# A trunk of two attention layers: the order of issue as a list of 3107 numbers

## Chip, cores and metric

The kernel runs on one core of a Trainium2 chip. A core has five engines that each work off a queue of their own in order: TensorE (PE, matrix products), VectorE (DVE), ScalarE (ACT), GpSimd (POOL), and SyncE (SP), which here only issues DMA transfers. The metric is the device time of one execution in microseconds (us), the median of several runs; smaller is better.

## What is computed

The reference takes a sequence of 256 rows of 1024 float32 numbers through two layers, each with a residual, and a final RMS norm:

```python
c_act = jax.nn.silu(c)
for layer in range(2):
    ada = einsum('bd,de->be', c_act, w_ada[layer]) + b_ada[layer]
    shift, scale, gate = split(ada, 3)
    h = rms_norm(x, norm_g[layer]) * (1 + scale) + shift
    y = even_mixer(h, ...) if layer == 0 else odd_mixer(h, ...)
    x = x + gate * y
return rms_norm(x, final_g)

def even_mixer(h, ...):     # one input projection of width 2968
    oa = swa_sink_attention(qa, ka, va, sinks) * silu(za)       # 8 heads, window 128
    ob = nsa_attention(qb, kc, vc, ks, vs, kw, vw, gb) * silu(zb)  # 8 heads, compressed + selected + window
    return concat(oa, ob) @ w_out

def odd_mixer(h, ...):      # one input projection of width 4096
    q, k, v, z = split(h @ w_in)
    return (moba_attention(q, k, v) * silu(z)) @ w_out          # 16 heads of 64
```

With 256 rows the selected blocks and the window of the second branch cover all past rows, and the odd layer's attention is causal over one block.

## The kernel before

Everything is float32. A weight is loaded as float32 into a buffer `raw` (five buffers, by SP's queue). ACT casts it to a rounded high half `whi`, DVE subtracts that from it for a low half `wlo`, and each projection is made of three fp32r products per tile of 128 rows of depth (`mm3`):

```python
T.matmul(o, shi, mhi, start=first, stop=False)
T.matmul(o, shi, mlo, start=False, stop=False)
T.matmul(o, slo, mhi, start=False, stop=last)
```

The activations are halved in the same way (`hhi`, `hlo` for the layer's input, `ghi`, `glo` for the gated attention output). Scores (`ps_s<-qT`), attention outputs (`ps_o<-pT,vb` and the like), and the sums of the condition (`ps_m<-cz,..`, `ps_m<-ones,acc`) are plain fp32 products, in part on subdivided tiles of the PE array. Transposes go by PE into the bank `ps_pt`, and ACT copies them out.

The first layer's input projection runs in eight groups over depth (`start_prep`, `start_mm`): each loads a slice of the condition's weights `w_ada` (into `qT` buffers and into `gate`), makes shift and scale of 128 features (`shs`), makes `hhi` and `hlo` for them, splits 128 rows of the projection's weights, and adds its products to seven banks. Then come the attention of the first layer, two heads at a time (`attn_pair`), with the gated projections (`gated`) and the condition's later parts in between, its output projection, the second layer's input projection and attention in quads of heads (`attn_quad`), and the output projection. The gate of a layer is made by DVE as a weighted sum of weight rows into `acc`, a product with ones on PE into `ps_m`, and an addition to `gate` on DVE (`ada_gate`).

The output of a layer goes through `add_scaled`: DVE multiplies the bank by `gate` (`t<-ps_pj,gate`), adds that to the residual `xs`, and sums the squares for the norm. At the end of the second layer the 256 rows are two tiles of 128; for each, POOL raises the mean square to the power −1/2 (`inv_root`, `parts`), ACT scales 384 columns and DVE 640 (`TENSOR_SCALAR t<-xs,parts`), and two transfers store them.

No operation is issued where it is written. `T`, `V`, `A`, `G` and `Y` stand for the five engines, and each call goes to `Plan.record`, which keeps it with the set of earlier operations that it depends on (overlaps of buffers and banks). The buffers of a ring are handed out while the operations are recorded. At the end `Plan.issue` emits all 3107 of them in the order that `Plan.order` returns; the waits between engines follow from the dependencies. `order` is a list scheduler: it estimates each operation's duration (`_cost`) and the delay between engines (`LAT`), ranks operations by the longest path behind them, places them forward in time (`_forward`), ranks them anew from a backward pass (`_backward`), and after twelve rounds keeps the order with the smallest estimated end. `plan.head` marks the SP transfers of the first stage, which stay in order of recording, and `groups` are sets of operations that get one common rank. Since all calls are made in `issue` through what `record` kept, nearly all rows of the profile have one line, L146.

Of the kernel before, what the change touches and what calls it, by code (L numbers as in the profile page):

```python
# [32 lines left out]
RAW, HIB, LOB = 5, 4, 4  # L33
INIT = 3e38

class _Engine:
# [10 lines left out]
class Plan:  # L49

    MIX = 1.0
    ROUNDS = 12
    COLD = 4200.0
    LAT = {
        "pe": {"pe": 0.0, "act": 197.0, "dve": 196.0, "pool": 270.0},
        "act": {"pe": 260.0, "act": 127.0, "dve": 131.0, "pool": 61.0},
        "dve": {"pe": 256.0, "act": 128.0, "dve": 127.0, "pool": 155.0},
        "pool": {"pe": 200.0, "act": 61.0, "dve": 60.0, "pool": 96.0},  # L60
    }

    def __init__(self, nc):
        self.ops = []
        self.acc = {}
        self.masks = {}
        self.after = {}
        self.groups = []
        self.head = 0
        self.tensor = _Engine(self, "pe", nc.tensor)  # L70
        self.vector = _Engine(self, "dve", nc.vector)
        self.scalar = _Engine(self, "act", nc.scalar)
        self.gpsimd = _Engine(self, "pool", nc.gpsimd)
        self.sync = _Engine(self, "sp", nc.sync)
# [21 lines left out]
    def _space(ap):  # L96
        return str(ap.space).split(".")[-1]

    @staticmethod
    def _n(ap):  # L100
        n = 1
        for d in ap.shape[1:]:
            n *= d
        return n

    def fence(self, key):

        self.after[key] = [i for i, o in enumerate(self.ops) if o["key"] == key][-1:]
# [1 line left out]
    def group(self, ids):  # L110

        deps = set().union(*(self.ops[i]["deps"] for i in ids)) - set(ids)
        for i in ids:
            self.ops[i]["deps"] = self.ops[i]["deps"] | deps
        self.groups.append(ids)

    def record(self, eng, name, args, kw):
        outs = [args[0]] if args else []
# [13 lines left out]
        for nm, b, w in uses:  # L132
# [7 lines left out]
                keep.append((ob, ow, oi))  # L140
            keep.append((b, w, i))
            self.acc[nm] = keep
        dur, dma = self._cost(eng.key, name, outs, ins, kw)
        real = eng.real
        self.ops.append(
            dict(key=eng.key, dur=dur, dma=dma, deps=deps, prio=i, fn=lambda: getattr(real, name)(*args, **kw))  # L146
        )
        return i

    def _cost(self, key, name, outs, ins, kw):  # L150
        o = outs[0]
        n = self._n(o)
        if name == "dma_start":
            return 0.0, n * o.shape[0] * 4 / 360.0
        if key == "pe":
            if name == "transpose":
                return 109.0, 0
            if "tile_position" in kw:
                f = o.shape[0] / 128 * ins[0].shape[0] / 128
                return n * 4 / 2.4 * f + (22 if o.shape[0] == 32 else 4), 0  # L160
            if str(ins[0].dtype).endswith("float32r"):
                return max(n / 2.4 + 4.5, 109.0), 0
            return max(n * 4 / 2.4 + 8, 218.0), 0
        src = max([self._n(a) for a in ins] + [n])
        psum = any(self._space(a) == "PSUM" for a in ins + outs)
        nap = sum(1 for a in ins[1:] if self._n(a) == 1 and n > 1)
        if key == "act":
            return 0.833 * n + (51 if psum else 93) + 93 * nap + (93 if "accum_out" in kw else 0), 0
        if key == "dve":
            if name in ("tensor_copy", "tensor_scalar"):  # L170
                return n * (1.04 if psum else 0.53) + 69 + 62 * nap, 0
            if name == "reciprocal":
                return 60 + 8.4 * n, 0
            if name == "memset":
                return 60 + 0.6 * n, 0
            return src * 1.04 + 70 + 62 * nap, 0
        return (150 + 2.1 * n if name == "tensor_tensor" else 140 + 1.25 * n), 0

    def _lat(self, a, b):
        return 0.0 if a["dma"] else self.LAT[a["key"]].get(b["key"], 100.0)  # L180

    def order(self):

        ops = self.ops
        n = len(ops)
        self.succ = succ = [[] for _ in range(n)]
        for i, o in enumerate(ops):
            for d in o["deps"]:
                succ[d].append(i)
        tail = [0.0] * n  # L190
        for i in range(n - 1, -1, -1):
            o = ops[i]
            t = o["dur"] + (o["dma"] + 2000.0 if o["dma"] else 0.0)
            for j in succ[i]:
                tail[i] = max(tail[i], tail[j] + self._lat(o, ops[j]))
            tail[i] += t
        top = max(tail)
        prio = [(1.0 - self.MIX) * o["prio"] * top / n + self.MIX * (top - tail[i]) for i, o in enumerate(ops)]
        best = None
        for _ in range(self.ROUNDS):  # L200
            for ids in self.groups:
                first = min(prio[i] for i in ids)
                for i in ids:
                    prio[i] = first
            start, end = self._forward(prio)
            if best is None or max(end) < best[0]:
                best = (max(end), start, end)
            prio = self._backward(end)
        _, start, end = best
        for i, o in enumerate(ops):  # L210
            o["start"], o["end"] = start[i], end[i]
        return sorted(range(n), key=lambda i: (start[i], i))

    def _backward(self, end):

        ops = self.ops
        n = len(ops)
        top = max(end)
        left = [len(q) for q in self.succ]
        avail = [0.0] * n  # L220
        late = [0.0] * n
        free = {k: 0.0 for k in ("pe", "act", "dve", "pool", "dma")}
        ready = {k: {} for k in free}
        kind = ["dma" if o["dma"] else o["key"] for o in ops]
        for i in range(n):
            if left[i] == 0:
                ready[kind[i]][i] = 0.0
        for _ in range(n):
            t0, k = min((max(free[k], min(rd.values())), k) for k, rd in ready.items() if rd)
            i = min((j for j, a in ready[k].items() if a <= t0), key=lambda j: (-end[j], -j))  # L230
            ready[k].pop(i)
            o = ops[i]
            if o["dma"]:
                free[k] = max(t0, avail[i] + 1400.0) + o["dma"]
                done = free[k] + 1450.0
            else:
                free[k] = done = t0 + o["dur"]
            late[i] = top - done
            for d in o["deps"]:
                avail[d] = max(avail[d], done + self._lat(ops[d], o))  # L240
                left[d] -= 1
                if left[d] == 0:
                    ready[kind[d]][d] = avail[d]
        return late

    def _forward(self, prio):
        ops, succ = self.ops, self.succ
        n = len(ops)
        left = [len(o["deps"]) for o in ops]
        free = {k: 0.0 for k in ("pe", "act", "dve", "pool", "sp")}  # L250
        ready = {k: {} for k in free}
        avail = [0.0] * n
        start = [0.0] * n
        ends = [0.0] * n
        hw_free, dma_free = 0.0, 1600.0
        for i in range(n):
            if left[i] == 0:
                ready[ops[i]["key"]][i] = 0.0
        fifo = [i for i in range(n - 1, -1, -1) if ops[i]["key"] == "sp" and i < self.head]
        for _ in range(n):  # L260
            now = dict(ready)
            if fifo:
                now["sp"] = {fifo[-1]: avail[fifo[-1]]} if left[fifo[-1]] == 0 else {}
            t0, k = min((max(free[k], min(rd.values())), k) for k, rd in now.items() if rd)
            i = min((j for j, a in now[k].items() if a <= t0), key=lambda j: (prio[j], j))
            t0 = max(free[k], ready[k].pop(i))
            o = ops[i]
            if k == "sp" and fifo:
                fifo.pop()
            if o["dma"]:  # L270
                if k == "pool":
                    free[k] = t0 + 1000.0
                    issued = t0 + 1600.0
                else:
                    free[k] = hw_free = max(hw_free, t0) + 450.0
                    issued = hw_free + 1000.0
                dma_free = max(issued, dma_free) + o["dma"]
                end = dma_free + 1400.0
            else:
                dur = 2 * o["dur"] if k == "pe" and t0 < self.COLD else o["dur"]  # L280
                free[k] = end = t0 + dur
            start[i], ends[i] = t0, end
            for j in succ[i]:
                avail[j] = max(avail[j], end + self._lat(o, ops[j]))
                left[j] -= 1
                if left[j] == 0:
                    ready[ops[j]["key"]][j] = avail[j]
        return start, ends

    def issue(self):  # L290
        for i in self.order():
            r = self.ops[i]["fn"]()
            self.ops[i]["inst"] = r


@with_exitstack
# [466 lines left out]
        start_mm(g, *prep)  # L763
        prep = nxt

    plan.head = len(plan.ops)
    Y.dma_start(tb, tbl_b[:, :1056])
    snk = const([P, 16], "snk")
    A.dma_start(snk[:, 0:8], a_sinks[0:1, :].to_broadcast([P, 8]))
# [553 lines left out]
```

## Time and profile before

| | us |
|---|---|
| median of three runs | 320.14 (319.93 to 320.33) |
| the profiled execution | 320.77 |
| its span, first to last instruction | 319.0 |
| PE busy | 302.2 |
| DVE busy | 265.7 |
| ACT busy | 186.2 |
| POOL busy | 12.4 |
| mean granted clock of TensorE | 0.985 |

The span is the time from the first to the last instruction in the profile; the execution's own time is a little longer. Busy times are sums over the instructions of one engine. Matmuls overlap in the pipeline, so the durations of neighbouring matmul rows overlap too, and the pace of PE is read from the distance of their starts.

### The profile page before, as it was taken

The numbers are of one execution on the slowest core, as the hardware profiler recorded it, in microseconds if no ns is written. First come the engines' busy times: TensorE is split into PE (matmuls) and PEld (weight loads), VectorE is DVE, ScalarE is ACT, GpSimd is POOL, SyncE is SP. The second block draws the span as 40 slices with busy tenths as digits, with TensorE's granted clock in tenths as the row PEclk, the third lists the DMA queues.
The fourth block names the chain that finished last, engine by engine and source line by source line (L and its number), as shares of the span: only waits on it lengthen the run. The fifth ranks groups of instructions, "written<-read, shape, count | busy, mean of one in ns | idle before, by whom it ended". The sixth has DMA issues, their size and how long they took to land.

```text
span 319.0 us, 6319 instructions
## 1 busy us (share of the span) xinstructions
PE 302.2 (95%) x2246; PEld 252.8 (79%) x2246; DVE 265.7 (83%) x744; ACT 186.2 (58%) x481; POOL 12.4 (4%) x30
## 2 busy tenths in 40 slices
PE   8599998989999999999999999999999999999990
PEld 8286876888677577788887789998999998987880
DVE  0369798899999999998899686689989969997854
ACT  5434336773665669978344785256645768773601
POOL 5000000001000000000001000000000000000102
PEclk9959999999999999999999999999999999999998
DMA  6999999998994796437599956726779443405003
GB/s 201 321 319 297 316 325 352 342 358 283 353 351 157 228 349 217 133 134 262 181 283 282 356 180 237 221 83 225 217 217 341 133 153 130 135 3 198 0 2 132
DMA packets 71280, 71.85 MB, mean 225 GB/s; under 512 B 3080, under 2 KB 62928, under 8 KB 71248
## 3 DMA queue, kind: packets, MB, share of 16 engines
q1 hardware_dynamic: 70528, 70.90, 70.1%
q10 hardware_dynamic: 592, 0.48, 0.5%
q8 instruction: 18, 0.29, 0.4%
q14 instruction: 14, 0.11, 0.1%
q0 software_dynamic: 128, 0.05, 0.1%
HBM read 70.38 MB, written 1.05 MB: 224 GB/s over the span
## 4 chain that ended last, share of the span: by engine, by line
PE 73%; DMA 13%; DVE 6%; ACT 2%; SPq 2%; issue 1%; POOL 0%; POOLq 0%; ACTq 0%
PE ps_pj L146 51%; PE ps_o L146 6%; PE ps_pt L146 6%; DMA gate<-in_w_ada_dram 6%; PE ps_s L146 6%; PE ps_m L146 4%; DMA qT<-in_w_ada_dram 4%; SPq L146 2%; DMA raw<-in_w_in_even_dram 2%; DVE t L146 2%; DMA ta<-in_tbl_a_dram 1%; DVE sm L146 1%; DVE acc L146 1%; DVE wlo L146 1%; ACT whi L146 1%
## 5 line engine op out<-in xcount | busy, mean ns | idle before, releaser
L146 ACT CAST whi<-raw 128x512 fp32r<-128x512 f32 (+1 forms) x132 | 74.9, 601 | 45.4 <-DMA raw<-in_w_in_even_dram 21.7
L146 DVE TENSOR_TENSOR wlo<-raw,whi 128x512 fp32r<-128x512 f32 (+1 forms) x116 | 73.9, 658 | 10.7 <-ACT whi L146 10.2
L146 PE MATMUL ps_pj<-hhi,wlo 128*128 128x256 f32 x256 | 63.2, 289 | 0.3 <-DVE wlo L146 0.3
L146 PE MATMUL ps_pj<-hhi,whi 128*128 128x256 f32 x256 | 62.9, 289 | 0.0
L146 PE MATMUL ps_pj<-hlo,whi 128*128 128x256 f32 x256 | 62.6, 289 | 0.0
L146 ACT ACTIVATE sm<-sm,mn 128x256 f32<-128x256 f32 (+1 forms) x76 | 34.1, 450 | 21.1 <-DVE mn L146 20.9
L146 PEld LDWEIGHTS ps_pj<-hhi,wlo 128*128 128x128 f32 x256 | 43.6, 188 | 2.4 <-issue 1.0
L146 PEld LDWEIGHTS ps_pj<-hhi,whi 128*128 128x128 f32 x256 | 43.3, 189 | 1.7 <-issue 1.0
L146 PEld LDWEIGHTS ps_pj<-hlo,whi 128*128 128x128 f32 x256 | 43.4, 188 | 0.7 <-issue 0.7
L146 DVE SCALAR_TENSOR_TENSOR acc<-raw,cz,acc 128x512 f32<-128x512 f32 x42 | 31.2, 744 | 0.0
L146 PE MATMUL ps_pj<-whi,hhi 128*128 128x512 f32 (+2 forms) x72 | 25.8, 389 | 1.7 <-ACT hhi L146 1.2
L146 PE MATMUL ps_pj<-whi,ghi 128*128 128x512 f32 (+1 forms) x72 | 26.5, 375 | 0.0
L146 PE MATMUL ps_pj<-wlo,hhi 128*128 128x512 f32 (+2 forms) x72 | 26.4, 385 | 0.0
L146 PE MATMUL ps_pj<-whi,glo 128*128 128x512 f32 (+1 forms) x72 | 26.3, 377 | 0.0
L146 PE MATMUL ps_pj<-wlo,ghi 128*128 128x512 f32 (+1 forms) x72 | 25.9, 371 | 0.0
L146 PE MATMUL ps_pj<-whi,hlo 128*128 128x512 f32 (+2 forms) x72 | 25.5, 373 | 0.0
L146 DVE SCALAR_TENSOR_TENSOR wlo<-raw,whi 128x512 fp32r<-128x512 f32 x32 | 20.6, 685 | 4.9 <-ACT whi L146 4.7
L146 PE MATMUL ps_pt<-ta,sm 128*128 128x128 f32 x114 | 23.7, 282 | 0.0
L146 DVE TENSOR_SCALAR sm<-sm,rc 128x128 f32<-128x128 f32 x76 | 20.3, 313 | 0.1
L146 ACT COPY pT<-ps_pt 128x384 f32<-128x384 f32 x33 | 15.5, 470 | 6.8 <-PE ps_pt L146 6.2
L146 PEld LDWEIGHTS ps_pj<-whi,hhi 128*128 128x128 f32 x72 | 13.5, 194 | 6.1 <-ACT whi L146 2.2
L146 PEld LDWEIGHTS ps_pt<-ta,sm 128*128 128x128 f32 x114 | 13.8, 142 | 4.7 <-issue 2.4
(206 smaller groups left out, 560.5 us busy)
## 6 DMA issues: line engine op xcount, KB each, us to landing
raw<-in_w_in_odd_dram SPq DMA_DIRECT2D x16, 1024.0 KB, 5.8
raw<-in_w_ada_dram SPq DMA_DIRECT2D x28, 512.0 KB, 5.8
qT<-in_w_ada_dram SPq DMA_DIRECT2D x24, 256.0 KB, 6.1
raw<-in_w_in_even_dram SPq DMA_DIRECT2D x5, 1024.0 KB, 7.1
raw<-in_w_in_even_dram SPq DMA_DIRECT2D x8, 576.0 KB, 5.6
raw<-in_w_out_even_dram SPq DMA_DIRECT2D x4, 1024.0 KB, 5.0
raw<-in_w_out_odd_dram SPq DMA_DIRECT2D x4, 1024.0 KB, 5.0
gate<-in_w_ada_dram SPq DMA_DIRECT2D x8, 256.0 KB, 5.8
```

Of the source, the lines that this page charges most:

```text
L146: dict(key=eng.key, dur=dur, dma=dma, deps=deps, prio=i, fn=lambda: getattr(real, name)(*args, **kw))
```

## The change

The scheduler, its cost estimates, `plan.head`, `groups` and the constants are removed. In their place stands a list `ORDER` of the numbers 0 to 3106, each the place of an operation in the order of recording, and `issue` emits the operations in that order. It asserts that every number occurs and that each operation comes behind all that it depends on. What is recorded stays the same: the operations, their operands, their buffers and their dependencies. In `group` only the line that kept the set for the scheduler goes.

```diff
+ORDER = [int(i) for i in """
+1 8 508 869 10 0 2 5 11 3 63 12 9 64 792 22 13 65 24 6 14 15 23 16 66 509 860 17 7 18 19 54 67 20 21 4 68 55 69
...
+3069 3077 3078 3042 3043 3079 3080 3081 3082 3070 3083 3044 3084 3085 3086 3071 3087 3088 3089 3090 3072 3091
+3073 3092 3093 3094 3095 3096 3097 3098 3099 3100 3101 3102 3103 3105 3104 3106
+""".split()]
...
-        dur, dma = self._cost(eng.key, name, outs, ins, kw)
         real = eng.real
-        self.ops.append(
-            dict(key=eng.key, dur=dur, dma=dma, deps=deps, prio=i, fn=lambda: getattr(real, name)(*args, **kw))
-        )
+        self.ops.append(dict(key=eng.key, deps=deps, fn=lambda: getattr(real, name)(*args, **kw)))
         return i
...
     def issue(self):
-        for i in self.order():
-            r = self.ops[i]["fn"]()
-            self.ops[i]["inst"] = r
+        place = {i: n for n, i in enumerate(ORDER)}
+        assert len(place) == len(ORDER) == len(self.ops)
+        for i in ORDER:
+            assert all(place[d] < place[i] for d in self.ops[i]["deps"])
+            self.ops[i]["inst"] = self.ops[i]["fn"]()
```

## Rows read from the trace of the kernel before

**Rows 1.** Page: busy time by engine, and the chain that ended last.

```profile
PE 302.2 (95%) x2246; PEld 252.8 (79%) x2246; DVE 265.7 (83%) x744; ACT 186.2 (58%) x481; POOL 12.4 (4%) x30
...
PE 73%; DMA 13%; DVE 6%; ACT 2%; SPq 2%; issue 1%; POOL 0%; POOLq 0%; ACTq 0%
```

**Rows 2.** Windows: busy time by engine, granted clock, DMA share, GB/s.

```profile
12.00:16.00 4.00, 2.05 (x21) 1.03 (x21) 1.57 (x5) 1.31 (x4) 0.00 (x0) 0.96 1.12 337
16.00:24.00 8.00, 7.73 (x26) 6.66 (x27) 5.40 (x14) 2.70 (x6) 0.00 (x0) 0.60 1.14 319
```

**Rows 3.** Chain in order of time: start, duration, what.

```profile
42.29 5.60 DMA raw<-in_w_in_even_dram
...
49.05 1.43 PE ps_pj L146 x5
```

**Rows 4.** Waits of PE, 49.1 to 311.4 us: total, times, longest.

```profile
PE ps_pj L146 <- ACT hhi L146: 1.2, 2, 1.0
PE ps_pt L146 <- ACT bigA L146: 0.8, 1, 0.8
PE ps_m L146 <- DVE hx L146: 0.7, 1, 0.7
PE ps_pj L146 <- DVE wlo L146: 0.3, 1, 0.3
```

**Rows 5.** Timeline of PE near 137 us: start, duration, instruction.

```profile
136.28 0.28 PE L146 MATMUL ps_pj<-hhi,wlo 128*128 128x256 f32 x1
136.49 0.87 PE L146 MATMUL ps_o<-pT,vb 128*64 128x256 f32 x8
137.29 0.51 PE L146 MATMUL ps_pj<-hhi,whi 128*128 128x256 f32 x2
137.64 0.40 PE L146 MATMUL ps_pj<-hlo,whi 128*128 128x256 f32 x2
137.87 0.28 PE L146 MATMUL ps_pj<-hhi,wlo 128*128 128x256 f32 x1
```

**Rows 6.** Timeline of PE, DVE and POOL at the end.

```profile
304.46 0.40 PE L146 MATMUL ps_pj<-whi,glo 128*128 128x512 f32 x1
...
307.41 0.69 DVE L146 TENSOR_TENSOR gate<-ps_m,gate 128x512 f32<-128x512 f32 x1 [3.88 <-PE ps_m L146]
...
311.16 0.99 POOL L146 TENSOR_TENSOR parts<-parts,expo 128x1 f32<-128x1 f32 x1
311.67 0.42 DVE L146 TENSOR_TENSOR t<-ps_pj,gate 128x256 f32<-128x256 f32 x1
...
312.19 0.55 DVE L146 TENSOR_SCALAR t<-xs,parts 128x640 f32<-128x640 f32 x1
312.65 0.42 DVE L146 TENSOR_TENSOR xs<-xs,t 128x256 f32<-128x256 f32 x1
```

**Rows 7.** Timeline of PE near 67 us.

```profile
67.72 0.55 PE L146 MATMUL ps_pt<-ta,bigA 128*128 128x128 f32 x3 [0.81 <-ACT bigA L146]
```

**Rows 8.** Timeline of ACT near 48 us.

```profile
47.97 0.62 ACT L146 CAST whi<-raw 128x512 fp32r<-128x512 f32 x1 [1.31 <-DMA raw<-in_w_in_even_dram]
48.49 0.50 ACT L146 ACTIVATE hhi<-oT,shs 128x256 fp32r<-128x256 f32 x1
```

**Rows 9.** Timeline of DVE near 48 us.

```profile
46.90 0.47 DVE L146 SCALAR_TENSOR_TENSOR oT<-bigA,shs,oT 128x256 f32<-128x256 f32 x1
...
48.62 0.69 DVE L146 TENSOR_TENSOR wlo<-raw,whi 128x512 fp32r<-128x512 f32 x1 [0.23 <-ACT whi L146]
```

**Rows 10.** Timeline of PE near 262 us: the trace's 1563rd place.

```profile
262.38 0.27 PE L146 MATMUL ps_pt<-ta,sm 128*128 128x128 f32 x1
```

**Rows 11.** Timeline of DVE near 268 us: the trace's 585th place.

```profile
267.56 0.42 DVE L146 CUSTOM_DVE_ANT_0 sm<-ps_m,tb 128x256 f32<-128x256 f32 x1
```

**Rows 12.** Windows, columns as in group 2.

```profile
210.00:240.00 30.00, 30.00 (x246) 26.82 (x245) 27.89 (x68) 16.63 (x40) 0.00 (x0) 1.00 0.63 195
240.00:290.00 50.00, 50.00 (x460) 45.74 (x460) 45.17 (x133) 36.29 (x99) 0.00 (x0) 1.00 0.43 146
```

More of the change, by code (lines that the diff above doesn't have):

```diff
@@ L49 @@
 class Plan:
[L53 to L61, printed above, removed]
     def __init__(self, nc):
@@ L67, in __init__ @@
         self.after = {}
-        self.groups = []
-        self.head = 0
         self.tensor = _Engine(self, "pe", nc.tensor)
@@ L97, in _space @@
         return str(ap.space).split(".")[-1]
[L99 to L104, printed above, removed]
     def fence(self, key):
@@ L114, in group @@
             self.ops[i]["deps"] = self.ops[i]["deps"] | deps
-        self.groups.append(ids)
     def record(self, eng, name, args, kw):
@@ L142, in record @@
             self.acc[nm] = keep
-        dur, dma = self._cost(eng.key, name, outs, ins, kw)
         real = eng.real
-        self.ops.append(
-            dict(key=eng.key, dur=dur, dma=dma, deps=deps, prio=i, fn=lambda: getattr(real, name)(*args, **kw))
-        )
-        return i
[L150 to L288, printed above, removed]
@@ L764, in tile_trunk @@
         prep = nxt
-    plan.head = len(plan.ops)
     Y.dma_start(tb, tbl_b[:, :1056])
```

128 rows, old and new, of the table ORDER are left out of this document.

## Prediction

> **What bounds the kernel now.** I read the page first. TensorE (PE) is busy 302.2 of 319.0 us, VectorE (DVE) 265.7, ScalarE (ACT) 186.2, and the chain that ended last runs through PE for 73% and through DMA for 13% [rows 1]. So the question for every stretch is whether PE had something to do.
>
> The windows and the chain of waits split the span in two. Up to about 48 us transfers set the pace: in 12 to 16 us the DMA engines are full (share 1.12, 337 GB/s), PE is busy 2.05 of 4 us [rows 2], and the chain hops from landing to landing of weight tiles, the last of them at 47.89 us (42.29 + 5.60), before PE takes over at 49.05 [rows 3]. After 49 us PE is the bound. The waits of PE from 49.1 to 311.4 us name only four releasers, 3.0 us in all [rows 4], and 1.0 of that is one stall, the one that ends at 49.05. What is left there is not a wait but a switch of kind: between two fp32r matmuls of 256 columns PE starts one every 0.115 us (137.64 to 137.87, two of them), but the step into a block of plain fp32 matmuls takes 0.21 (136.28 to 136.49), and the two matmuls behind the block take 0.35 instead of 0.23 (137.29 to 137.64) [rows 5]. One visit to plain fp32 so costs 0.10 on entry and 0.12 on exit, about 0.2 us, beyond its own work.
>
> Behind the last matmul comes a serial tail of DVE, GpSimd (POOL), ACT and the last store, 311.67 us to the end [rows 6].
>
> **What the change does.** No instruction is added or removed, and no dependency or buffer is changed: the ring buffers were handed out when the operations were recorded. Only the place of an operation in its engine's queue changes. I counted that by laying the list over the order that the trace shows: of PE's 1879 recorded operations 1758 stand elsewhere, of DVE's 660 594, of ACT's 398 336, of POOL's 26 12, of SyncE's (SP) 144 transfers 36.
>
> **The terms.**
>
> 1. Fewer visits to plain fp32. Counted along PE's queue, the trace enters a plain fp32 block 63 times from fp32r or from transposes, the list 56 times: some attention outputs stand as one block of eight instead of two of four, and a gate's matmul stands beside another. 7 x 0.2 = 1.4 us less. Bounds: if a joined block still pays one side, 7 x 0.1 = 0.7, and 7 x 0.22 = 1.5. The row is of just such a block, so I take 1.4.
>
> 2. The stall that ends at 67.72 us. PE stood idle for 0.81 us until ACT had copied the input of a transpose [rows 7]. In the list six fp32r matmuls of the same projection, which the trace has behind this transpose, stand ahead of it: 6 x 0.115 = 0.7 us of work put into the hole. Bounds 0 (their weights are late) and 0.81; I take 0.7.
>
> 3. The stall before 49.05. ACT took the weight cast at 47.97, when its tile had landed, and only behind it the ACTIVATE that makes `hhi`, at 48.49; PE waited for that until 49.05 [rows 8, 3]. In the list the ACTIVATE stands ahead of the cast. Its own input `oT` was done by 47.37 (46.90 + 0.47) [rows 9], so it ends before the tile lands, and PE waits for the cast alone, which ends at 48.59. From ACTIVATE's end to PE's start is 0.06 us (48.99, 49.05), so PE starts at about 48.7: 0.3 to 0.4 us sooner, I take 0.3.
>
> 4. Against it: the list runs the three products of a bank back to back far more often (successive matmuls of one bank 1117 times, in the trace 633), so in the DMA-fed stretch the low half `wlo`, made by DVE from the cast tile, is wanted three or four matmuls into a group, where the trace has seven or eight matmuls that need only the high half. Near 49 us the list also queues one more accumulation ahead of a `wlo` on DVE; it has the form of the 0.47 us row, the `wlo` takes 0.69 [rows 9]. Bounds 0 (PE has high-half work for as long) and 0.8 (the 0.47, and half of a `wlo`); I take +0.4, near the accumulation's 0.47.
>
> 5. The tail. In the trace the scaling of the first half's output (TENSOR_SCALAR, 312.19) sits on DVE between the last gate product (311.67) and the last addition to `xs` (312.65) [rows 6]. The product issues at 311.67 and lasts 0.42, so without the scaling the addition could start near 312.15. In the list the scaling stands three DVE operations sooner. All that follows the addition (sum of squares, POOL's power, the last scaling, the store) moves with it: −0.5 us. The scaling reads POOL's power, which ended at 312.15 (311.16 + 0.99), and a DVE operation that waits holds back those queued behind it, the last product among them; so the new place pays only if the power is early. It is: in the trace the first half's own product stood on DVE behind the addition of `gate`, which waited 3.88 us for PE's `ps_m` and ran from 307.41 to 308.10, although the last matmul of that half's bank was issued at 304.46 [rows 6]. The list has `ps_m` about 200 of its 3107 places sooner (2841 against 3048), so the first half's product can start near 305 (304.46, 0.40 for the matmul) instead of 308.1, and its power is done about 3 us sooner, near 309. Bounds 0 (the scaling waits after all) and 0.5.
>
> 6. Transfers. The first 68 SP issues are the same, so the stretch to 48 us gets its weights in the same order. Later mostly neighbours are swapped; the bias row set of `gate` (0.5 MB) moves ahead of the compression weights. PE waits for no transfer after 49.1 [rows 4], so I cost this at nothing; without that cover it is 0.5 MB at the 337 GB/s of rows 2, 1.6 us.
>
> 7. Everything else that trades places behind a busy PE: nothing, as long as PE always finds its next operands ready. It is the assumption that the rivals attack.
>
> Sum: −1.4 − 0.7 − 0.3 + 0.4 − 0.5 = −2.5 us on the span, 319.0 to 316.5. The profiled execution took 320.77 (1.77 beyond the span) and the median of the runs is 320.14, 0.63 lower; so the profile would say 318.3 and the median **317.6 us**. A change within 0.2% (0.64 us, 319.5 to 320.8) can't be told from none.
>
> **Rivals.**
>
> A. Slower: PE's queue asks too early. PE runs in order, so an operand that is late stops everything behind it. The place to look is the odd layer's attention. The three transposes of a probability tile that the trace runs from 270.83 us stand in the list at PE's 1563rd place, which the trace reached at 262.4 us [rows 10]. Their last input is a DVE scaling, and it stands at DVE's 585th place, which the trace reached at 267.56 us [rows 11]. Measured by places DVE would come about 5.6 us after PE asked (the operation at that place ends at 268.0). For it: DVE is busy 45.17 of 50 us in 240 to 290 [rows 12] and has little room. Against it: places are not times, and DVE's idle time ahead of it can be used up: 2.1 us in 210 to 240 alone [rows 12]. 5.6 − 2.1 = 3.5 us of new waits, +1.0 on the span with the other terms, median 321.1. It decides above 2.5 us of new waits (no gain), above 3.1 it is slower. Chance 0.12.
>
> B. Gains given back. The same mechanism at 2 to 3 us, or terms 1, 2 and 5 at their lower ends (0.7 + 0 + 0.3 + 0 − 0.8 = 0.2): 319.5 to 320.8, middle 320.0. Chance 0.15.
>
> C. Larger. All 3.0 us of PE's waits in rows 4 go, with 1.5 for the blocks, 0.5 for the tail and about 0.5 for small gaps that have no releaser: 5.5 us, 314.6. Terms 2 and 3 are inside the 3.0. Nothing in the list shows that the waits for `hx` (0.7) get covered, so chance 0.13 for anything below 316.3.
>
> D. The clock. TensorE's granted clock fell to its lower level of 1.2 GHz after 16 us, after PE had been busy only 2.05 of the 4 us before, and 16 to 24 us had 0.60 of the full clock [rows 2]. If the tighter wait of term 4 thins PE's work out late in the DMA-fed stretch, the fall is repeated there: 8 x 0.40 = 3.2 us of full-speed work lost, +0.7 with the rest, median 320.8 or more. It decides if PE idles there as it did in 12 to 16 us. Chance 0.06. The Trainium skill states this mechanism (TensorE: Matmul & The Clock Gate, HAM oscillation): a kernel that waits for DMA between groups of matmuls can have its clock throttled again, and each group starts cold. By that rule alone every DMA-fed group would be at risk; the rows agree with it at 12 to 24 us, where there was one fall.
>
> E. The list only writes down what the scheduler found, so nothing changes. Excluded: the scaling of rows 6 stands after the last gate product in the trace, and before it in the list.
>
> **How the numbers follow.** The forecast (316.3 to 318.9 by the bounds of its terms) has 0.54, C 0.13, B 0.15, A 0.12, D 0.06. Faster by over 0.2% is the forecast and C, 0.67; within 0.2% is B, 0.15; slower is A and D, 0.18. The range goes from C's end, 314.6, to just beyond D and most of A, 321.1.
>
> **What would show it.** Right: 56 visits to plain fp32 and the PE waits after 49 us under 2 us; no empty PE between 66 and 68 us beyond 0.4 us; PE's restart near 48.7 us; `xs` about 0.5 us after the last gate product starts. Wrong: PE waits on DVE `sm` or on ACT's copies of transposed tiles in 210 to 280 us (A); a granted clock of 0.5 after 24 us (D); a last `xs` that still starts a microsecond after the product, because the scaling waited for POOL (term 5 at nothing, or worse).

## The result and the profile after

The changed kernel takes 319.09 us, the median of 20 runs (317.62 to 320.21); the kernel before took 320.44 us in the same comparison (20 runs, 319.58 to 322.28). The ratio is 0.9947 (95% interval 0.9931 to 0.9963): faster, by 1.2 to 2.2 us. The forecast was 317.6 us, 2.5 us faster; the direction is right, the size is a little over half (1.35 us by the medians, 1.7 by the ratio).

The profile makes it look better than the median. The profiled execution took 317.62 us, the fastest of the 20, with a span of 315.8 against 319.0; the profile of the kernel before is one of its middling runs (320.77). The fastest run of each, 317.62 and 319.58, are 2.0 us apart, not 3.2. Busy time and chain on the page after (compare [rows 1]):

```profile
PE 300.0 (95%) x2246; PEld 251.0 (79%) x2246; DVE 271.1 (86%) x744; ACT 189.9 (60%) x481; POOL 12.3 (4%) x30
...
PE 57%; DVE 22%; DMA 9%; ACT 4%; issue 4%; SPq 2%; POOL 1%; POOLq 0%; ACTq 0%; DVEq 0%
```

TensorE does the same matmuls in 2.2 us less busy time, so the gain is not only in waits. VectorE is 5.4 us busier with the same instructions. The waits of TensorE from 49.1 to 311.4 us are 1.7 us in all, where they were 3.0 [rows 4]:

```profile
PE ps_s L256 <- DVE mn L256: 0.6, 1, 0.6
PE ps_m L256 <- DVE vz L256: 0.5, 1, 0.5
PE ps_pt L256 <- DVE hx L256: 0.4, 1, 0.4
PE ps_s L256 <- ACT t L256: 0.2, 1, 0.2
```

Of the 1.3 us less, 1.0 is the one stall that ended at 49.05 us. The waits for `mn` and `vz`, 1.2 us together, are new; they stand at 82 and 88 us:

```profile
82.04 0.93 PE L256 MATMUL ps_s<-kTb,qT 64*128 64x128 f32 x8 [0.63 <-DVE mn L256]
...
88.42 0.66 PE L256 MATMUL ps_m<-w2v,hr 128*128 128x64 f32 x4 [0.54 <-DVE vz L256]
```

The hole at 67 us is gone. TensorE's timeline there, where [rows 7] had 0.81 us of idle time, shows no wait:

```profile
66.21 0.39 PE L256 MATMUL ps_pj<-wlo,hhi 128*128 128x256 f32 x1
...
66.92 0.61 PE L256 MATMUL ps_o<-ta,bigA 128*128 128x128 f32 x4
67.37 0.63 PE L256 MATMUL ps_pt<-ta,bigA 128*128 128x128 f32 x4
67.76 0.36 PE L256 MATMUL ps_pj<-whi,hhi 128*128 128x256 f32 x1
```

ScalarE has made `hhi` before it waits for the next weight tile, and casts as soon as that has landed (compare [rows 8]):

```profile
45.24 0.51 ACT L256 ACTIVATE hhi<-oT,shs 128x256 fp32r<-128x256 f32 x1 [2.17 <-DVE oT L256]
45.65 0.30 ACT L256 CAST whi<-raw 128x152 fp32r<-128x152 f32 x1
47.53 1.90 ACT L256 CAST whi<-raw 128x512 fp32r<-128x512 f32 x3 [1.57 <-DMA raw<-in_w_in_even_dram]
```

And at the end VectorE runs the first half's scaling (306.77) before the last product (308.96), whose addition follows after 0.46 us and not after 0.98 [rows 6]:

```profile
303.29 0.69 DVE L256 TENSOR_TENSOR t<-ps_pj,gate 128x512 f32<-128x512 f32 x1 [0.91 <-PE ps_pj L256]
...
306.77 0.56 DVE L256 TENSOR_SCALAR t<-xs,parts 128x640 f32<-128x640 f32 x1
...
308.96 0.42 DVE L256 TENSOR_TENSOR t<-ps_pj,gate 128x256 f32<-128x256 f32 x1 [0.16 <-PE ps_pj L256]
309.42 0.43 DVE L256 TENSOR_TENSOR xs<-xs,t 128x256 f32<-128x256 f32 x1
```

**Where the time went, by places.** Every operation of both orders can be found in the traces, so both can be cut at the same places of the order. Places 520, 1000, 1300 and 1960 are near 62, 104, 131 and 201 us; the two orders have issued nearly the same operations by 520 and by 1960 (2 of them differ), by 1000 they differ in 25 and by 1300 in 17. What one order has done by 1000 and the other not yet takes TensorE nearly the same time both ways (by 1000 it is 2.6 us each in the changed kernel's trace and 3.2 against 3.5 in that of before, by 1300 0.9 each in the former), so the stretches can be compared. The table gives the time between the ends of the last TensorE operation before each cut, worked out from the traces of all kernels of this study, good to 0.1 us. Order L is the list, O the order before.

| kernel | to 520 | 520 to 1000 | 1000 to 1300 | 1300 to 1960 | 1960 to last product | behind it | span |
|---|---|---|---|---|---|---|---|
| before | 62.2 O | 42.3 O | 27.0 O | 70.2 O | 109.7 O | 7.6 O | 319.0 |
| after | 62.0 L | 42.1 L | 25.3 L | 69.9 L | 109.6 L | 6.9 L | 315.8 |
| list_again | 62.2 L | 42.1 L | 27.1 L | 70.2 L | 110.6 L | 6.9 L | 319.1 |
| list_start | 63.4 L | 42.4 O | 27.0 O | 70.6 O | 109.7 O | 7.6 O | 320.7 |
| old_start | 62.6 O | 42.1 L | 25.4 L | 70.4 L | 109.5 L | 6.9 L | 316.9 |
| list_from95 | 61.7 L | 43.6 L | 25.3 L | 70.6 L | 109.5 L | 7.0 L | 317.7 |
| ta_first | 61.6 L | 42.0 L | 25.4 L | 70.8 L | 109.5 L | 6.9 L | 316.2 |
| old_start_hhi | 64.0 O | 43.6 L | 25.3 L | 70.2 L | 109.5 L | 7.0 L | 319.6 |
| list_mid | 61.5 O | 43.2 L | 26.2 L | 70.6 L/O | 109.8 O | 7.6 O | 318.9 |
| list_end | 62.6 O | 42.3 O | 27.2 O | 70.6 O | 109.9 L | 6.9 L | 319.5 |
| tail_only | 61.3 O | 42.3 O | 27.5 O | 71.2 O | 109.7 O/L | 7.0 L | 319.0 |
| mid_tail | 64.4 O | 42.3 O | 29.2 L | 72.5 O | 109.7 O/L | 6.9 L | 325.0 |
| old_to1000 | 63.8 O | 42.3 O | 29.2 L | 70.5 L | 109.5 L | 7.0 L | 322.3 |
| switch20 | 62.3 L | 43.7 L | 27.1 L | 71.6 L | 112.9 L | 6.9 L | 324.5 |

So the list's gain in the profiles sits in two places: 1.7 us between places 1000 and 1300, and 0.7 us behind the last product. Only the second is there in every profile. The first is there in five (25.3 and 25.4); list_mid has 26.2 and list_again 27.1 with the same order, and experiment 12 says why. The other stretches give 0.1 to 0.3 each, less than the same order differs from itself. The last three rows have edits or cuts inside a stretch (experiments 8, 10 and 11).

### The profile page after: what moved, and what is told of

It is laid out like the page before. It is cut to its first block, busy times and chain, and to the rows that moved or that the text cites. A ratio compares the mean times of both kernels' runs of the same rounds, so it can differ in the third digit from the quotient of the medians.

```text
span 315.8 us, 6311 instructions
## 1 busy us (share of the span) xinstructions
PE 300.0 (95%) x2246; PEld 251.0 (79%) x2246; DVE 271.1 (86%) x744; ACT 189.9 (60%) x481; POOL 12.3 (4%) x30
## 4 chain that ended last, share of the span: by engine, by line
PE 57%; DVE 22%; DMA 9%; ACT 4%; issue 4%; SPq 2%; POOL 1%; POOLq 0%; ACTq 0%; DVEq 0%
PE ps_pj L256 41%; DVE t L256 5%; DVE acc L256 5%; PE ps_pt L256 5%; PE ps_s L256 5%; PE ps_o L256 5%; DVE wlo L256 4%; DVE sm L256 4%; PE ps_m L256 2%; SPq L256 2%; DMA qT<-in_w_ada_dram 2%; DMA gate<-in_w_ada_dram 2%; DMA snk<-in_a_sinks_dram 2%; DMA raw<-in_w_in_even_dram 2%; DMA raw<-in_w_in_odd_dram 2%
## 5 line engine op out<-in xcount | busy, mean ns | idle before, releaser
L256 ACT CAST whi<-raw 128x512 fp32r<-128x512 f32 (+1 forms) x132 | 76.4, 600 | 47.4 <-PE ps_pj L256 28.9
L256 PE MATMUL ps_pj<-hhi,whi 128*128 128x256 f32 x256 | 73.0, 289 | 0.0
L256 PE MATMUL ps_pj<-hhi,wlo 128*128 128x256 f32 x256 | 72.2, 285 | 0.0
L256 PE MATMUL ps_pj<-hlo,whi 128*128 128x256 f32 x256 | 72.0, 283 | 0.0
L256 PEld LDWEIGHTS ps_pj<-hhi,whi 128*128 128x128 f32 x256 | 47.9, 188 | 1.4 <-issue 0.8
L256 PEld LDWEIGHTS ps_pj<-hlo,whi 128*128 128x128 f32 x256 | 48.1, 188 | 0.7 <-issue 0.3
L256 PEld LDWEIGHTS ps_pj<-hhi,wlo 128*128 128x128 f32 x256 | 47.9, 188 | 0.5 <-issue 0.2
L256 ACT ACTIVATE sm<-sm,mn 128x128 f32<-128x128 f32 (+1 forms) x76 | 34.1, 450 | 12.0 <-DVE mn L256 11.9
L256 DVE TENSOR_SCALAR sm<-sm,rc 128x256 f32<-128x256 f32 (+1 forms) x76 | 21.8, 318 | 0.3
L256 PE MATMUL ps_pt<-ta,sm 128*128 128x128 f32 x114 | 20.4, 280 | 0.0
```

What stands on the lines that cost most here:

```text
L256: self.ops.append(dict(key=eng.key, deps=deps, fn=lambda: getattr(real, name)(*args, **kw)))
```

## The experiments

Since the operations are the same, an experiment can be an order put together from the two: the first n places of one, and then all that is left in the sequence of the other. Dependencies stay kept by that.

**1. The list only at the start.**

```diff
-ORDER = list
+head = list[:520]
+ORDER = head + [i for i in old if i not in head]
```

> The list for the first 520 places (to about 62 us), the old order behind them. At that seam the profiles stand at 61.9 us (old) and 61.6 us (list), but the list's runs spread over 2.6 us with granted clocks of 0.976 to 0.992, and the profile was its fastest. Theory M (the gain lies behind 62 us, the start of the list costs time on most runs): 0.7 to 1.3 us slower than before. Rival S (the start gives the gain, since the clock fell before the first group's products): 1 us faster. Rival N (the start is neutral): within 0.4 us.

322.07 us against 320.81 (ratio 1.0017, 0.9987 to 1.0046). No gain, so S falls; whether there is a cost (M) or none (N) the interval leaves open. Its profile needed 63.4 us to place 520, the slowest list start of six.

**2. The old start and the list behind it.**

```diff
+head = old[:520]
+ORDER = head + [i for i in list if i not in head]
```

> The old order for the first 520 places, the list behind them. Theory M: all of the gain of rows read behind 62 us, 2.3 to 2.9 us faster than before, so faster than the list itself. Rival S: at most 0.7 us faster. Rival N: as the list, 1.3 to 1.7 us faster.

318.66 us against 320.81 (0.9898, 0.9856 to 0.9941; 6 runs): the whole gain is there without the list's start. That it is better than the list itself isn't shown, the intervals touch.

**3. The list only from 520 to 1625.**

```diff
+head = old[:520]
+part = (head + [i for i in list if i not in head])[:1625]
+ORDER = part + [i for i in old if i not in part]
```

> The list only from place 520 to 1625 (62 to 165 us), the old order around it. In the profiles the list gains 1.8 us between these seams. Theory M: 1.6 to 2.0 us faster than before: the hole at 67 us 0.7, five of the seven visits to plain fp32 that are saved 1.0. Rival (the gain is spread evenly over the kernel): 0.5 us faster.

320.23 us against 320.81 (0.9953, 0.9920 to 0.9986), 1.5 us by the ratio: near M's value, but the interval (0.4 to 2.6 us) holds the rival's 0.5 too, and the medians are only 0.6 us apart. Its profile is less good than its ratio: between 84 and 88 us TensorE's clock was down (0.57), as in experiment 5, and between 1000 and 1300 a weight tile came late, as in experiment 12.

**4. The list only from 1960.**

```diff
+head = old[:1960]
+ORDER = head + [i for i in list if i not in head]
```

> The list only from place 1960 (201 us) to the end. In the profiles PE gains 0.2 us there and the tail behind its last product 0.7. Theory M: 0.6 to 1.0 us faster. Rival (new waits of DVE scalings in the odd layer eat what the tail gives): within 0.3 us of before.

321.63 us against 320.81 (1.0010, 0.9978 to 1.0042): the rival's value lies in the middle of the interval, M's 0.6 us just inside its edge (0.7), so neither falls. The profile shows the tail at 6.9 us, and little lost between 1960 and the last product (109.9 against 109.7). The rest of what its span has over that of the kernel before lies in stretches whose order is the old one (62.6, 27.2 and 70.6 us).

**5. The old order for the first 95 places only, and 6. the list with its first transfers in the old order.**

```diff
+head = old[:95]
+ORDER = head + [i for i in list if i not in head]
```

```diff
-... 508 ... 0 ... 3 ...    (sinks, condition, table: ScalarE's queue)
+... 3 ... 0 ... 508 ...
```

> The old order for the first 95 places only (to about 12 us: first transfers, transposes of the input, first shift and scale), the list behind them. In the list ScalarE's queue issues the table with the identity third, TensorE waits 2.6 us for it at 8.7 us, and the first projection product starts at 17.9 us where the trace of before has 17.1. Theory E (that late table is what the list's start costs): first product back at 17.0 to 17.4 us, time as with the old start to place 520, 2.0 to 3.0 us under before. Rival W (the low halves wanted earlier in the groups, places 95 to 520): as the list, 1.3 to 1.7 us under before.

> The list with one edit: of the three transfers at the head of ScalarE's queue the table goes first, then the condition, then the sinks. Theory E: the wait of 2.6 us for the table becomes under 1 us, the first product comes 0.4 to 0.9 us sooner, the time is 0.4 to 0.9 us under the list's. Rival W: the wait goes, and the time stays the list's within 0.3 us, since weights land no sooner.

318.61 us (0.9925, 0.9903 to 0.9948) and 318.19 us (0.9915, 0.9895 to 0.9935), both against 321.18. The first product starts at 17.52 and 17.28 us, where the list has 17.88. By the ratios that is 2.4 and 2.7 us under before, as E says; W's 1.7 is at the very edge of the first interval. The medians are 0.5 and 0.9 us under the list's, as E says for the second. But the list was timed in other sessions, and its intervals (0.9931 to 0.9963, and 0.9926 to 0.9973 in experiment 12) overlap both, so E is likely and not shown. Place 520 comes at 61.7 and 61.6 us, with the list at 62.0 and 62.2; the old order by itself spreads from 61.3 to 64.4.

What list_from95 did show is in its windows between 80 and 96 us (busy times, granted clock, DMA share, GB/s):

```profile
80.00:84.00 4.00, 2.97 (x32) 1.71 (x24) 4.00 (x14) 2.84 (x9) 0.00 (x0) 1.00 1.00 317
84.00:88.00 4.00, 3.58 (x33) 3.15 (x32) 3.82 (x20) 3.19 (x10) 0.00 (x0) 1.00 1.09 365
88.00:92.00 4.00, 3.74 (x32) 3.17 (x32) 3.95 (x16) 1.44 (x6) 0.00 (x0) 1.00 1.07 339
92.00:96.00 4.00, 4.00 (x24) 2.47 (x24) 3.81 (x16) 3.10 (x10) 0.00 (x0) 0.61 0.45 132
```

The granted clock is 0.61 in 92 to 96 us: for most of these 4 us it is at its lower level of 1.2 GHz, and TensorE gets 24 matmuls done instead of the 35 of the changed kernel's own profile, which has the same order and waits of the same lengths here:

```profile
88.00:92.00 4.00, 3.43 (x29) 2.86 (x29) 3.93 (x17) 1.44 (x5) 0.00 (x0) 1.00 1.10 348
92.00:96.00 4.00, 4.00 (x35) 3.18 (x35) 4.00 (x15) 3.39 (x10) 0.00 (x0) 1.00 0.48 138
```

Of the eight profiles that run the list between places 520 and 1000, four have such a fall between 84 and 100 us (list_from95, list_mid, old_start_hhi, switch20), and these need 43.2 to 43.7 us for the stretch; the four others need 42.0 to 42.1. Of the six that run the old order there none has a fall (42.3, list_start 42.4). So in this stretch the list can lose 1.1 to 1.6 us that the old order did not lose in any profile; four of eight against none of six is little to go by, and switch20 also has two visits more there. The old order has a fall of its own elsewhere: at 48 to 56 us in three of the eight profiles that start with it (old_start_hhi, mid_tail and old_to1000, granted clock 0.72 to 0.86 in these windows). They reach place 520 at 63.8 to 64.4 us, the five others at 61.3 to 62.6. None of the six profiles with the list's start, in whole or from place 95, has that fall.

**7. The old start with one ACTIVATE moved.**

```diff
 ORDER of experiment 2:
-... 346 (cast) ... 342 (hhi) ...
+... 342 (hhi) 346 (cast) ...
```

> The old order to place 520 and the list behind it, with one operation moved: the ACTIVATE that makes hhi of the seventh group stands ahead of the weight cast on ScalarE, four places sooner. Theory (term 3 of the forecast): the product behind it waits for the cast and not for hhi, 0.3 to 0.5 us sooner than a landing plus 1.1 us; 0.3 us under the old start without the edit. Rival: the transfer sets the end of that stage anyway, nothing changes.

319.19 us against 321.18 (0.9931, 0.9897 to 0.9965). TensorE waits for the cast and no longer for `hhi`, as the theory says, but the waits at 47.87 and 49.74 us then are for weights, 0.51 and 1.15 us:

```profile
47.87 0.73 PE L256 MATMUL ps_pj<-whi,hhi 128*128 128x512 f32 x2 [0.51 <-ACT whi L256]
49.74 0.45 PE L256 MATMUL ps_pj<-whi,hhi 128*128 128x408 f32 x1 [1.15 <-ACT whi L256]
```

The interval overlaps that of experiment 2, so the 0.3 us is neither shown nor refuted as time; the rival fits the profile better.

**8. Twenty more visits to plain fp32.** The list with 20 fp32r products put into the middle of plain fp32 blocks that they followed.

```diff
-... s1 s2 s3 s4 s5 s6 s7 s8  p1 p2 p3 ...     (s: scores, p: projection)
+... s1 s2 s3 s4  p1  s5 s6 s7 s8  p2 p3 ...
```

> The list with 20 more visits to plain fp32 on TensorE (76 in place of 56): 20 fp32r products that stand just behind a plain fp32 block are put into its middle. Nothing else moves. Theory (0.2 us a visit): 4.0 us over the list, about 323. If only one side of a visit is paid: 2.0 us over it. Rival (the order of kinds is free, the gain is from waits): as the list.

325.83 us against 321.18 (1.0146, 1.0119 to 1.0173). Against the list's 0.9947 that is 1.0146 − 0.9947 = 2.0% or 6.4 us, 0.32 us a visit (0.25 to 0.39 by the ends of the two intervals): the rival falls, and the price is more than the 0.2 of the theory. Timeline of TensorE at one of them, and of the changed kernel at the same scores without it:

```profile
208.00 0.28 PE L256 MATMUL ps_s<-qT 32*128 32x128 f32 x2
...
208.22 0.39 PE L256 MATMUL ps_pj<-hlo,whi 128*128 128x256 f32 x1
208.53 0.38 PE L256 MATMUL ps_s<-qT 32*128 32x128 f32 x2
```

```profile
202.63 0.28 PE L256 MATMUL ps_s<-qT 32*128 32x128 f32 x2
...
202.74 0.28 PE L256 MATMUL ps_s<-qT 32*128 32x128 f32 x2
```

From scores to scores it is 0.11 us without the product between (202.63 to 202.74) and 0.53 with it (208.00 to 208.53). The product's own 0.115 taken off, the visit costs 0.53 − 0.11 − 0.115 = 0.31 us. Taken in the same way from both traces, the twenty cost 0.1 to 0.33 us each, most of them 0.3, and 5.5 us in all (0.27 on average). These are single products put into a block; that a visit which the list saves is worth as much is taken over from them and was not tested by itself.

**9. The tail alone.**

```diff
 old order:
+2853 (product with ones for the last gate part) and 2854 (its addition) directly behind 2716
+the last 117 places in the sequence of the list
```

> The old order with two things taken from the list: the product of the last gate part and its addition stand before the last projection, and the last 150 places run as in the list, so the first half's scaling stands ahead of the last product on VectorE. Theory (term 5): from the last TensorE product to the end 6.9 us in place of 7.6, 0.7 us faster than before. Rival: the product with ones only moves into another wait of TensorE, no gain.

The edit sets the sequence of the last 117 places; in the last 150, of which the expectation speaks, the same operations stand as in the list. 320.75 us against 320.63 (0.9989, 0.9962 to 1.0015). The interval holds the 0.7 us of the theory and zero. The profile shows 7.0 us behind the last product, 7.6 before, as all eleven profiles with the list's tail do (6.9 to 7.0).

**10. Tail and places 1000 to 1300, and 11. the old order to place 1000.**

```diff
 experiment 9, and between the cuts:
+head = old[:1000]
+part = (head + [i for i in list if i not in head])[:1300]
+then old
```

```diff
+head = old[:1000]
+ORDER = head + [i for i in list if i not in head]
```

> As tail_only, and the list also between places 1000 and 1300 (104 to 131 us), where the profiles show 13 visits to plain fp32 in the old order and 8 in the list. Theory (the list's lasting gain is five visits there and the tail): 1.7 + 0.7 = 2.4 us faster than before, as much as the list or more. Rival (the gain is spread over the whole list): 1.0 us.

> The old order to place 1000 (104 us, the stretch in which transfers run without a break), the list behind it. Theory (what the list does before 104 us gains nothing and costs some on most runs): 2.4 to 2.8 us faster than before, 0.8 to 1.2 under the list. Rival (the hole at 67 us and others before 104 us matter): 1.0 to 1.7 us faster.

Both miss by far: 326.57 us (1.0165, 1.0117 to 1.0213) and 324.03 us (1.0077, 1.0045 to 1.0108), against 320.63. What they measure is in good part the cut. By place 1000 the two orders have issued 25 different operations each, and what one has done and the other not yet is caught up behind the cut, in places where its results are late. Two of TensorE's waits in experiment 10 show it, one behind each of its cuts; the first, 1.23 us, is the same in experiment 11:

```profile
108.36 0.70 PE L256 MATMUL ps_m<-asb,selbc 128*128 128x256 f32 x2 [1.23 <-ACT asb L256]
...
138.93 0.39 PE L256 MATMUL ps_pj<-hhi,whi 128*128 128x256 f32 x1 [2.25 <-ACT whi L256]
```

The stretch from 1000 to 1300 took 29.2 us in both, more than in either order by itself (27.0 and 25.3). Both profiles have a fall of the clock in 48 to 56 us besides, with the old order. They don't speak for or against the theory; that the gain can be had from this stretch alone was not shown.

**12. The list once more.**

> The changed kernel itself, for a comparison in one session with the others and a second profile of it: 1.3 to 1.9 us faster than before. Theory: its profile shows the same 25.3 us between places 1000 and 1300 and 6.9 us behind the last product, and what differs from the first profile lies before 104 us.

319.12 us against 320.63 (0.9950, 0.9926 to 0.9973): the first result again. Its profile (320.86 us) took 27.1 us from 1000 to 1300, so the expectation that it would differ ahead of 104 us only is wrong. ScalarE waited there 2.03 us for a weight tile that landed late, and TensorE for the copy queued behind the cast:

```profile
111.80 0.62 ACT L256 CAST whi<-raw 128x512 fp32r<-128x512 f32 x1 [2.03 <-DMA raw<-in_w_in_even_dram]
```

```profile
116.01 0.55 PE L256 MATMUL ps_pt<-ta,sm 128*128 128x128 f32 x3 [1.20 <-ACT pT L256]
```

The changed kernel's first profile has no such wait with the same order, but by a narrow margin: the tile was issued at 104.13 us, landed at 109.29, and its cast began at 109.45. In list_again it was issued at 104.33 and landed at 111.72, 7.4 us after its issue and not 5.2; DMA moved 306 and 315 GB/s between 96 and 104 us there, 359 and 342 in the first profile. In list_mid ScalarE waited 1.07 us for the same tile, in old_start 0.34. The order leaves that transfer no room.

## Why the prediction was right, and where its sum was off

**The bound and the rule of the sum** held: no instruction changed, and what changed is TensorE's steps between kinds and its waits. The profile of the fastest run gives 3.2 us on the span, the forecast was 2.5. That the sum came out near is in part luck: a visit was priced too low, and a gain and several losses that it had at other sizes or at nothing cancel. The forecast's interval is also not the one that its terms give: with all of them at their better bounds the sum is −3.2 us, at their worse bounds −0.2, so 316.9 to 319.9 and not 316.3 to 318.9. The measured 319.09 lies in the former, and just outside the latter.

**Term 1 (visits, −1.4)** was right in kind and too small in price. A visit costs 0.31 us and not 0.2. The forecast counted the slow step into the block and the slow second product behind it; it missed that the step from the last plain fp32 matmul to the first fp32r product is slow too (208.00 to 208.22, 0.22 us, where the next scores would have come after 0.11). Counted by places the visits don't fall everywhere: 26 before place 1000 become 31, 13 from 1000 to 1300 become 8, and 24 behind it become 17. The 1.7 us between 1000 and 1300 has the size of five visits at 0.31 (1.6), an account by count that experiments 10 and 11 were to test and did not. The seven fewer behind place 1300 gave 0.4 us in the first profile, less than 2.2; what takes the rest there was not found.

**Term 2 (the hole at 67 us, −0.7)**: the hole is filled, but the stretch from 520 to 1000 is only 0.2 us shorter (42.3 to 42.1). TensorE's waits in it are 1.8 us before (`bigA` 0.81, `hx` 0.74, `wlo` 0.27) and 1.6 after (`mn` 0.63, `vz` 0.54, `hx` 0.40): the list fills one hole and opens two others a little later. It also has two visits more (15 to 17), 0.6 us at the price above.

**Terms 3 and 4 (−0.3, +0.4)**: The products that began at 49.05 us [rows 3] begin at 48.60, against 48.7 forecast, and without a stall ahead of them: low-half products of the group before, which the list runs later, fill it. Place 520 is reached at 62.0 and 62.2 us with the list and at 62.2 before, near the +0.1 of the two terms together. But TensorE's waits for `wlo` up to 62 us are 0.4 us before and after, so term 4's cost did not show as a wait; those for `hhi` are 1.0 and 0.7, term 3's size. The late table was not in the sum: TensorE stands 2.63 us for it at 8.74 us, and the first product comes 0.8 us later (17.88, before 17.12); by place 520 nothing is left of it.

**Term 5 (the tail, −0.5)** was 0.7. The last addition starts 0.46 us after the product, as forecast (0.5), and the product itself comes 0.31 us after the start of the last matmul (308.65 to 308.96), where it came after 0.55 (311.12 to 311.67), since VectorE is free by then.

**Terms 6 and 7 (transfers and everything else at nothing)** are the step that failed: "nothing, as long as PE always finds its next operands ready". Even in the fastest run the new waits for `mn` and `vz` are 1.2 us. And term 6 took the absence of waits for transfers in the trace of before as room, where the list leaves none: in list_again one tile landed late and cost 1.8 us between 1000 and 1300, and a VectorE result cost 0.7 us at 247 us.

**Rival D (the clock)** had the right mechanism in the wrong place. It put the fall into the transfer-fed start and gave it 0.06. The first fall, at 16 to 24 us [rows 2], moved about from run to run (8 to 12 us in the changed kernel's profile, 16 to 24 in list_again's), and place 520 was reached at the same time. The falls that cost are the one at 84 to 100 us, 1.1 to 1.6 us in four of eight profiles with the list there, and the old start's at 48 to 56 us. In the 20 runs of the changed kernel the 12 with a mean granted clock above 0.980 have a median of 318.47 us, the 8 others 319.75: 1.3 us, the size of one such fall. How many of the 20 had it can't be read from a mean clock, so this part is argued, not shown.

**Rival A (attention asks too early)** did not come: from place 1960 to the last product it is 109.5 to 109.9 us with either order, but for list_again and the edited switch20. **Rival B** (gains given back) had the mechanism that did come, queues that ask too early, and put it at 2 to 3 us; the new waits of TensorE are 1.2 us in the first profile, more in list_again. **Rival C** did not come: no run of the list is below 317.62 us, and of TensorE's waits 1.7 us are left. **Rival E** was rightly excluded.

Taken together: the spans of the two profiles are 3.2 us apart, the fastest runs 2.0, the medians 1.35, and the ratio gives 1.7. A fall of the clock of 1.1 to 1.6 us or a late tile of 1.8 us in a part of the list's runs would make up such a difference, with falls of the old order's on the other side. How often each comes was not measured, so this account is argued.

## What to carry to other kernels

An added visit to another kind of matmul costs TensorE time without any wait, so an order of issue may gain by visiting less often; price the whole round trip, both steps and the first product behind it, from an added visit rather than from one edge. A hole that is filled gives its time only where the new order opens no other behind it. A transfer that nobody waits for in one order says nothing of its room in another: read from landing to use. One profile can be the best of 20 runs: before a gain is read from it, cut the traces of several kernels at the same places of the order and look at which stretches agree. And an order pieced together from two is a clean experiment only where both have issued nearly the same operations; at a cut with 25 different ones the cut itself cost 2 us and more.

## What was not expected of the hardware

The clock fell in the middle of the kernel with no wait for a transfer on TensorE: in list_from95 its waits between 76 and 98 us are 0.6, 0.5 and 0.4 us, and it was 2.97, 3.58 and 3.74 of 4 us busy in the three windows ahead of the fall, part of that in plain fp32 matmuls of 32 to 256 columns. The changed kernel's own profile, with 2.97, 3.88 and 3.43 and the same three waits, kept its full clock. With nearly the same work the clock fell in one run and not in the other, and these rows don't tell why. The Trainium skill describes falls that come from frequent, very short idle gaps between groups of matmuls, in a kernel that cycles through PSUM banks (TensorE: Matmul & The Clock Gate, A second HAM failure mode: psum-queue depth-cycling). No run here shows that this is the cause: the profile that kept its clock has the same waits.
